# Two attention mixers of a transformer block on one NeuronCore: heads handled in pairs instead of one by one, and two weight staging buffers instead of three

## The chip, the cores and the metric

The kernel runs on one core of a Trainium2 chip. The metric is the time of one execution on the device, in microseconds (us). All data are float32, for a sequence of 512 tokens and a model width of 1024.

## What is computed

Two stacks are run one after the other, each of two layers. The change touches the mixer of the first stack alone. There a normed input `h` goes through one wide projection into queries, keys and values of two mixers and into gates:

```python
qa, ka, va, qb, kb, vb, gate_pre = jnp.split(h @ w_in[l], splits, axis=-1)
o_a = dilated_mixture(...)            # 12 heads of 64: 3 groups (window, dilation) x 4 slots
o_b = stick_breaking_attention(...)   # 4 heads of 64
merged = g_a * (o_a @ w_br[l, :OUT_A]) + g_b * (o_b @ w_br[l, OUT_A:])
```

Stick-breaking attention has no softmax. For a query t and a key s < t the weight is `sigmoid(z_ts) * prod(1 - sigmoid(z_tj))` over the keys j between them, so a running product along the keys is needed. The dilated mixture is softmax attention in three patterns, whose outputs are joined per slot by their softmax sums. The rest of the block is the output projection, a gated feed-forward net with a short convolution, and then the second stack (gated linear attention, differential attention, a Fourier mix and a feed-forward net, on the 512 tokens and, in part, on 256 context tokens).

## The kernel before

**Projections.** Nearly all the time goes into projections of weights that stream from HBM. `load_weights` (L116) brings each tile of 1024 columns x 128 rows of float32 (512 KB) into a buffer of the pool `raw` (L55, three buffers; L125, issued on SyncE's queue, SP). ScalarE then rounds it into `whi` (L126, three buffers), and VectorE writes the rest, `raw - whi`, into `wlo` (L127, two buffers); after that the `raw` buffer is free. `mm3` (L131 to L135) makes one product of three matmuls, `whi` by the input's high part, `whi` by its low part, `wlo` by its high part. `proj_t` (L137) does that for eight blocks of the contraction: 24 matmuls of 512 columns for one weight tile. `weights` (L106) asks for the next tile of a recorded plan while the current one is used.

**The mixer** (`mixer1`, L269) projects the stick-breaking queries and keys (L318, L319), then values (L328), then the twelve query and key tiles of the dilated mixture (L333, L334), then more values (L335). Then come the heads, one at a time: for each of four values of `s`, `stick(s)` (L536) and `dsw(s)` (L467). After them the softmax sums are exchanged through DRAM (`dsw_join`, L506), the outputs are transposed (`heads_t`, L561), sixteen gate tiles are projected (L351 to L360), and the branch projections begin (L366).

**stick** goes through four blocks of 128 queries. For each it makes a score matmul with a contraction of 64, from the upper or the lower half of the partitions (L545, `sc`), tanh on ScalarE (L547), then on VectorE a mask, the stay factors, a running product and the weights (L549 to L556), then transposes the weights block by block (L458, `at`), copies them out, on ScalarE or VectorE in turn (`evac`), and multiplies them with the values, with the transposed weights as the stationary side and 64 columns of values as the moving side (L464, `po`). **dsw** does the same with three scores for each of four query blocks (L478), a fused add-and-minimum and an exp (L487, L488), transposes (L494) and products with 65 columns of values (L500).

**Order.** The kernel gives only dependences and a program order. A scheduler in the framework fixes each engine's order at build time: on TensorE the next ready instruction, earliest in the program first. So the gate projections (`mm<-h`) stand between the heads' matmuls. Engines then run their queues in that fixed order. The banks of PSUM in this stage are `mm` 2, `sc` 3, `at` 2 and `po` 1 (L264). float32 matmuls that are not split appear in the trace as two records each, transposes as one.

Of the kernel before, what the change touches and what calls it, by code (L numbers as in the profile page):

```python
# [10 lines left out]
F32 = mybir.dt.float32  # L11
F32R = mybir.dt.float32r
U8 = mybir.dt.uint8
AF = mybir.ActivationFunctionType
ALU = mybir.AluOpType
# [3 lines left out]
P = 128  # L19
# [28 lines left out]
class Net:  # L48
    def __init__(self, ctx, tc, io, plan):
        self.plan, self.asked, self.ahead = plan, [], []  # L50
        self.tc, self.nc, self.io = tc, tc.nc, io
        pool = lambda name, bufs, **kw: ctx.enter_context(tc.tile_pool(name=name, bufs=bufs, **kw))
        self.pc = pool("const", 1)
        self.px = pool("resid", 1)
        self.praw = pool("raw", 3)  # L55
        self.pw = pool("wsplit", 1)
        self.ps = pool("tmp", 4)
        self.psm = pool("small", 4)
        self.n = 0
        self.consts()  # L60
# [19 lines left out]
    def tmp(self, name, n=T, dt=F32):  # L80
        if n <= TC:
            return self.ps.tile([P, n], dt, tag="th", name=self.nm(name), bufs=4)
        return self.ps.tile([P, n], dt, tag="t", name=self.nm(name))
# [147 lines left out]
    def token_factor(self, acc, classes=False):  # L231


        bc, r = self.rstd_bcast(acc, 4, D)
        if classes:
            r = r, self.rstd_cols(acc, 4, D, classes=True)
        out = self.pv1.tile([P, T], F32, tag="fac", name=self.nm("fac"), bufs=1)
        self.nc.scalar.copy(out, bc)
        return out, r
# [18 lines left out]
    def block1(self, layers, ctx=True):  # L258
        self.x = []
        with self.scope(pa=("act", 16), pv1=("factor", 1)):  # L260
            self.vec1 = self.pv1.tile([P, self.io["vec1"].shape[1]], F32, tag="vec1", name="vec1", bufs=1)
            self.nc.sync.dma_start(self.vec1, self.io["vec1"])
            for l in range(layers):
                with self.scope(pk=("work", 3), pv=("vals", 1), banks={"mm": 2, "sc": 3, "at": 2, "po": 1}):  # L264
                    acc = self.mixer1(l, None if l else "load")
                with self.scope(pmod=("mod", 2), banks={"mm": 6, "at": 2}):
                    self.ffn1(l, acc, ctx and l == layers - 1)

    def mixer1(self, l, first):  # L269
        nc, io = self.nc, self.io  # L270
        ready = []
        if first:
# [3 lines left out]
            for i in range(4):  # L276
                w = self.weights(io["w_in_t"][l, 12 + i], KT, P)
                if i == 0:
                    self.load_x(1, KT)
                    self.h1 = [self.gained(l, "norm1", k) for k in range(KT)]  # L280
                if i == 2:
                    for k in range(KT):
                        self.sumsq(self.acc1, self.x[k], k == 0)
                    self.load_consts()
                    fac, rcs = self.token_factor(self.acc1, True)
                ps = self.bank("mm" if i < 2 else "sc")
                self.proj_t(ps, w, 0, self.h1)
                ready.append(ps)
# [3 lines left out]
        self.nw = 0  # L292
# [33 lines left out]
        banks = ("mm", "mm", "sc", "sc")  # L326
# [6 lines left out]
        qa = proj_qk(0, 6, 0.125)  # L333
        ka = proj_qk(6, 6, 1.0)  # L334
        for ps in self.wide(io["w_in_n"][l, 1], hs, [slice(b, T, 4) for b in range(4)], banks):  # L335
            pass
        for b in range(4):
            nc.scalar.mul(va[1][b][:, :, 0:64], heads(ps[b]), rcs[1][:, b:b + 1])

        ob = [self.pv.tile([P, 256], F32, tag=f"ob{b}", name=self.nm("onat")) for b in range(4)]  # L340
# [3 lines left out]
        for s in range(4):  # L344
            self.stick(s, qb, kb, vb, ob)
            self.dsw(s, qa, ka, va, sums, stat)
        on, last = self.dsw_join(sums, stat)
        ob = self.heads_t(ob, "o")
# [17 lines left out]
        for c in range(4):  # L366
            w = self.weights(io["w_br"][l, c], 4, 256)
            for j in range(2):
                n = 2 * c + j
                pa, pb = self.bank("sc"), self.bank("sc")  # L370
# [80 lines left out]
    def weighted(self, out, blocks, width):  # L451

        nc = self.nc
        for b0 in range(0, len(blocks), 4):
            grp = blocks[b0:b0 + 4]
            pt = self.bank("at")
            for i, (p_, v) in enumerate(grp):
                nc.tensor.transpose(pt[:, i * P:(i + 1) * P], p_, self.ident)  # L458
            pT = self.tmp("pT")
            n = len(grp) * P  # L460
            self.evac(self.nw, pT[:, :n], pt[:, :n])
            self.nw += 1
            for i, (p_, v) in enumerate(grp):
                nc.tensor.matmul(out[:, :width], pT[:, i * P:(i + 1) * P], v,  # L464
                                 start=b0 + i == 0, stop=b0 + i == len(blocks) - 1)

    def dsw(self, s, qa, ka, va, sums, stat):  # L467
# [3 lines left out]
        bias = self.pk.tile([P, 512], F32, tag="bias", name=self.nm("bias"), bufs=2)  # L471
        nc.sync.dma_start(bias, self.io["dswb"][s])
        for b in range(4):
            k0 = max(b - 1, 0) * P
            n0 = (b + 1) * P - k0
            r = 64 * (s % 2)
            ps = self.bank("sc")
            mm = lambda out, g, q, k: nc.tensor.matmul(out, qa[2 * g + s // 2][r:r + 64, q], ka[2 * g + s // 2][r:r + 64, k],  # L478
                                                       start=True, stop=True)
            own = slice(b * P, (b + 1) * P)  # L480
            mm(ps[:, 0:n0], 0, own, slice(k0, (b + 1) * P))
            for g in (1, 2):
                mm(ps[:, (g + 1) * P:(g + 2) * P], g, own, own)
            e = self.pk.tile([P, 512], F32, tag="e", name=self.nm("e"), bufs=2)
            for c, (sl, bi) in enumerate(((slice(0, n0), bias[:, 256 - n0:256]), (slice(256, 512), bias[:, 256:512]))):
                nm = stat[:, c, b, 0, s:s + 1]
                nc.vector.tensor_tensor_reduce(e[:, sl], ps[:, sl], bi, -1.0, 3.0e38, ALU.add, ALU.min, accum_out=nm)  # L487
                nc.scalar.activation(e[:, sl], e[:, sl], AF.Exp, bias=nm, scale=-1.0)  # L488
            blocks = [(0, e[:, i * P:(i + 1) * P], va[0][k0 // P + i][:, s, :]) for i in range(n0 // P)]
            blocks += [(1, e[:, (g + 1) * P:(g + 2) * P], va[1][b][:, 4 * (g - 1) + s, :]) for g in (1, 2)]  # L490
            n = len(blocks) * P
            pt = self.bank("at")
            for i, (_, p_, _) in enumerate(blocks):
                nc.tensor.transpose(pt[:, i * P:(i + 1) * P], p_, self.ident)  # L494
            pT = self.tmp("pT")
            self.evac(self.nw, pT[:, :n], pt[:, :n])
            self.nw += 1
            po = self.bank("po")
            for i, (c, _, v) in enumerate(blocks):
                nc.tensor.matmul(po[:, 65 * c:65 * (c + 1)], pT[:, i * P:(i + 1) * P], v,  # L500
                                 start=i in (0, len(blocks) - 2), stop=i in (len(blocks) - 3, len(blocks) - 1))
            po = po[:, 0:130].rearrange("p (c d) -> p c d", c=2)
            nc.scalar.copy(sums[b][:, :, s, :], po[:, :, 0:64])
            nc.vector.tensor_copy(stat[:, :, b, 1, s:s + 1], po[:, :, 64:65])
# [31 lines left out]
    def stick(self, h, qb, kb, vb, on):  # L536

        nc = self.nc  # L540
        j, r = h // 2, 64 * (h % 2)
        for qi in range(4):
            kw = (qi + 1) * P
            pz = self.bank("sc")
            nc.tensor.matmul(pz[:, :kw], qb[j][r:r + 64, qi * P:kw], kb[j][r:r + 64, 0:kw], start=True, stop=True)  # L545
            y = self.tmp("y")
            nc.scalar.activation(y[:, :kw], pz[:, :kw], AF.Tanh, scale=0.5)  # L547
            d = y[:, qi * P:kw]
            nc.vector.tensor_tensor(d, d, self.smask, ALU.min)  # L549
            g = self.pk.tile([P, T + 2], F32, tag="stay", name=self.nm("stay"), bufs=1)  # L550
            nc.gpsimd.memset(g[:, 0:1], 1.0)
            nc.vector.tensor_scalar(g[:, kw:0:-1], y[:, :kw], -0.5, 0.5, ALU.mult, ALU.add)
            c = self.tmp("left")
            nc.vector.tensor_tensor_scan(c[:, :kw], g[:, 0:kw], g[:, 0:kw], 1.0, ALU.mult, ALU.bypass)
            rev = c[:, kw - 1::-1] if kw == T else c[:, 0:kw][:, ::-1]
            nc.vector.scalar_tensor_tensor(y[:, :kw], y[:, :kw], 1.0, rev, ALU.add, ALU.mult)  # L556
            po = self.bank("po")
            self.weighted(po, [(y[:, i * P:(i + 1) * P], vb[:, i, h * 64:(h + 1) * 64]) for i in range(qi + 1)], 64)
            nc.scalar.copy(on[qi][:, h * 64:(h + 1) * 64], po[:, 0:64])

    def heads_t(self, on, name, classes=None):  # L561

        out = []
        for j in range(2):
            pts = []
            for part in (on, classes) if classes else (on,):
                pt = self.bank("at")
# [911 lines left out]
    def block2(self):  # L1479
        st = Stream("l", T, 0, self.x)  # L1480
        st.acc = self.acc1
        with self.scope(pcx=("ctx", 1), psm=("small2", 4)):
# [188 lines left out]
```

## Time and profile before

| | |
|---|---|
| three timed runs | 3258.72, 3259.57, 3263.57 us; median 3259.57 |
| the profiled execution | 3259.87 us, of which the span of the instructions is 3258.1 us |
| TensorE matmul, weight load | 98%, 82% of the span |
| VectorE, ScalarE, GpSimd | 62%, 42%, 2% |
| granted TensorE clock, mean | 0.996 of full speed |
| HBM | 367.57 MB, 113 GB/s over the span |

Busy time is the time in which an engine has at least one instruction in flight. Matmuls are pipelined, so the duration of one (about 390 ns for 512 columns) is longer than the distance from its start to the next one's start; distances of starts are what an instruction costs TensorE. A row of the timeline is a run of like instructions: start, length from the first start to the last end, engine, line, operation, tiles, shape and count.

### The profile page before, as it was taken

How to read it: one execution, taken by the hardware profiler on the slowest of the kernel's cores; microseconds unless marked ns; L12 is line 12 of the kernel's file. 1: busy time of each engine (PE TensorE's matmuls, PEld its weight loads, DVE VectorE, ACT ScalarE, POOL GpSimd, SP SyncE). 2: the span in 40 equal slices, each digit the busy share in tenths (PEclk: the TensorE clock that was granted, in tenths of full speed). 3: DMA queues.
4: the chain of work that ended last, by engine and by line, in shares of the span. 5: the costliest groups of instructions: out<-in, count | busy, mean ns of one | idle time of the engine just before them, and what ended most of it. 6: DMA issues, size and time to landing. Idle time of an engine off the chain costs nothing.

```text
span 3258.1 us, 46766 instructions
## 1 busy us (share of the span) xinstructions
PE 3196.9 (98%) x18808; PEld 2684.9 (82%) x18808; DVE 2009.5 (62%) x3320; ACT 1353.8 (42%) x2304; POOL 68.7 (2%) x213
## 2 busy tenths in 40 slices
PE   9999999999999999999999999999999999999998
PEld 7878888888878888889778788888898778888887
DVE  4366799663456799667767775333266677653335
ACT  3244433242234433346647654222244467542223
POOL 0000000000000000000100000000000100000000
PEclk9999999999999999999999999999999999999999
DMA  4213466433213466436242234332134522222333
GB/s 141 84 40 117 132 202 216 130 104 91 81 37 117 148 204 210 136 106 193 86 131 75 59 111 138 95 97 91 57 117 131 168 78 71 76 80 93 97 95 117
DMA packets 109226, 370.62 MB, mean 114 GB/s; under 512 B 13264, under 2 KB 18384, under 8 KB 109008
## 3 DMA queue, kind: packets, MB, share of 16 engines
q1 hardware_dynamic: 103824, 352.28, 34.8%
q0 software_dynamic: 5184, 15.34, 1.7%
q8 instruction: 148, 2.42, 0.3%
q14 instruction: 70, 0.57, 0.1%
HBM read 359.64 MB, written 7.93 MB: 113 GB/s over the span
## 4 chain that ended last, share of the span: by engine, by line
PE 91%; DVE 3%; ACT 3%; DMA 2%; issue 1%; SPq 0%; DVEq 0%; ACTq 0%
PE mm L133 24%; PE mm L135 24%; PE mm L134 24%; PE at L1258 2%; PE sc L478 1%; PE po L500 1%; PE ds L1236 1%; DVE wlo L127 1%; PE mm L170 1%; PE mm L171 1%; PE mm L172 1%; DMA raw<-w_in2v 1%; ACT whi L126 1%; PE sc L545 1%; PE at L1254 1%
## 5 line engine op out<-in xcount | busy, mean ns | idle before, releaser
L126 ACT CAST whi<-raw 128x1024 fp32r<-128x1024 f32 (+1 forms) x556 | 575.9, 1036 | 1194.3 <-PE mm L134 793.4
L127 DVE TENSOR_TENSOR wlo<-raw,whi 128x1024 fp32r<-128x1024 f32 (+1 forms) x556 | 666.8, 1200 | 317.3 <-PE mm L135 175.8
L133 PE MATMUL mm<-h,whi 128*128 128x512 f32 x1904 | 753.3, 396 | 12.4 <-ACT whi L126 7.9
L135 PE MATMUL mm<-h,wlo 128*128 128x512 f32 x1904 | 753.2, 396 | 0.1
L134 PE MATMUL mm<-h,whi 128*128 128x512 f32 x1904 | 750.2, 394 | 0.0
L133 PEld LDWEIGHTS mm<-h,whi 128*128 128x128 f32 x1904 | 358.6, 188 | 85.3 <-issue 7.9
L135 PEld LDWEIGHTS mm<-h,wlo 128*128 128x128 f32 x1904 | 358.2, 188 | 74.8 <-DVE wlo L127 2.0
L134 PEld LDWEIGHTS mm<-h,whi 128*128 128x128 f32 x1904 | 358.3, 188 | 71.5 <-issue 1.1
L135 PE MATMUL mm<-hid,wlo 128*128 128x512 f32 (+1 forms) x896 | 324.7, 363 | 3.2 <-DVE wlo L127 3.1
L133 PE MATMUL mm<-hid,whi 128*128 128x512 f32 (+1 forms) x896 | 324.9, 363 | 0.4 <-ACT whi L126 0.4
L134 PE MATMUL mm<-hid,whi 128*128 128x512 f32 (+1 forms) x896 | 325.0, 363 | 0.0
L135 PEld LDWEIGHTS mm<-hid,wlo 128*128 128x128 f32 x896 | 168.8, 189 | 31.4 <-DVE wlo L127 3.8
L133 PEld LDWEIGHTS mm<-hid,whi 128*128 128x128 f32 x896 | 168.8, 189 | 28.3 <-ACT whi L126 0.6
L134 PEld LDWEIGHTS mm<-hid,whi 128*128 128x128 f32 x896 | 168.9, 189 | 27.9 <-DVE hid L180 0.4
L133 PE MATMUL mm<-cat,whi 128*128 128x512 f32 (+1 forms) x512 | 187.1, 367 | 4.6 <-ACT cat L701 3.3
L135 PE MATMUL mm<-cat,wlo 128*128 128x512 f32 (+1 forms) x512 | 186.8, 366 | 0.0
L134 PE MATMUL mm<-cat,whi 128*128 128x512 f32 (+1 forms) x512 | 186.4, 365 | 0.0
L1399 DVE TENSOR_TENSOR silu<-silu,mm 128x512 f32<-128x512 f32 (+1 forms) x58 | 36.1, 623 | 223.2 <-PE mm L135 222.7
L674 DVE SCALAR_TENSOR_TENSOR junk<-wmod,c 128x1024 f32<-128x1024 f32 x96 | 116.8, 1217 | 4.2 <-DMA wmod<-w_mod 3.7
L674 DVE SCALAR_TENSOR_TENSOR wmod<-wmod,c 128x1024 f32<-128x1024 f32 x96 | 116.8, 1217 | 0.7
L133 PEld LDWEIGHTS mm<-cat,whi 128*128 128x128 f32 x512 | 97.4, 191 | 20.5 <-ACT cat L701 3.6
L134 PEld LDWEIGHTS mm<-cat,whi 128*128 128x128 f32 x512 | 97.2, 190 | 15.1
(484 smaller groups left out, 5166.8 us busy)
## 6 DMA issues: line engine op xcount, KB each, us to landing
raw<-w_fi SPq DMA_DIRECT2D x120, 512.0 KB, 3.6
wmod<-w_mod SPq DMA_DIRECT2D x96, 512.0 KB, 4.2
raw<-w_up SPq DMA_DIRECT2D x88, 512.0 KB, 3.7
raw<-w_in2t SPq DMA_DIRECT2D x76, 512.0 KB, 3.6
raw<-w_in_t SPq DMA_DIRECT2D x64, 512.0 KB, 3.6
raw<-w_fo SPq DMA_DIRECT2D x48, 512.0 KB, 3.6
raw<-w_down SPq DMA_DIRECT2D x32, 512.0 KB, 3.7
raw<-w_out SPq DMA_DIRECT2D x28, 512.0 KB, 3.6
```

What stands on the lines that cost most here:

```text
L126: nc.scalar.copy(hi, raw)
L127: nc.vector.tensor_tensor(lo, raw, hi.bitcast(F32), ALU.subtract)
L133: mm(out, lh, rh, start=start, stop=False)
L134: mm(out, lh, rl, start=False, stop=False)
L135: mm(out, ll, rh, start=False, stop=stop)
L170: mm(out[i], xh, hi, start=k == 0, stop=False)
L171: mm(out[i], xh, lo, start=False, stop=False)
L172: mm(out[i], xl, hi, start=False, stop=k == last)
L478: mm = lambda out, g, q, k: nc.tensor.matmul(out, qa[2 * g + s // 2][r:r + 64, q], ka[2 * g + s // 2][r:r + 64, k], start=True, stop=True)
L674: ins = nc.vector.scalar_tensor_tensor(o, w, 1.0, cs[v], ALU.mult, ALU.mult, accum_out=self.mods[l][v][:, j:j + 1])
L1258: mm(po[:, 0:64], wT[:, i * P:(i + 1) * P], vals[c0 + i][:, h * 64:(h + 1) * 64], start=c0 + i == 0, stop=c0 + i == nkb - 1)
L1399: nc.vector.tensor_tensor(s, s, ps[1][:, :n], ALU.mult)
```

## The change

- `raw` has two buffers, not three.
- `stick` and `dsw` take two heads at a time, `j` in 0, 1. The two heads' score matmuls are issued in turn, one contracting over partitions 0 to 63, the other over 64 to 127, and write two neighbouring banks of PSUM (`pair_bank`, 1024 columns).
- In `stick` the elementwise steps cover both heads in one instruction, except for the running product, which is one instruction for each head, in place. The transposed weights are now the moving side (128 columns), the values the stationary side (64 columns), and the two heads write partitions 0 to 63 and 64 to 127 of one bank. The result is already transposed, so `heads_t` isn't called for it.
- `dsw` keeps its count of score, transpose and value instructions.
- The banks are `mm` 2, `sc` one pair, `at` one pair, `po` 2. Work tiles `y` have two buffers, shared by `stick` and `dsw`; `stay`, `pT` and `bias` have one.
- The second set of values is projected before the query and key tiles of the dilated mixture. The copy of the token factor comes before the column sums by class.

The diff without moves of small pools and without the removed bodies, which are printed above:

```diff
@@ -52,7 +52,7 @@
-        self.praw = pool("raw", 3)
+        self.praw = pool("raw", 2)
@@ -232,10 +232,10 @@
+        out = self.pv1.tile([P, T], F32, tag="fac", name=self.nm("fac"), bufs=1)
+        self.nc.scalar.copy(out, bc)
...
-        out = self.pv1.tile([P, T], F32, tag="fac", name=self.nm("fac"), bufs=1)
-        self.nc.scalar.copy(out, bc)
@@ -261,9 +261,9 @@
-                with self.scope(pk=("work", 3), pv=("vals", 1), banks={"mm": 2, "sc": 3, "at": 2, "po": 1}):
+                with self.scope(pk=("work", 1), pv=("vals", 1), banks={"mm": 2, "sc": 1, "at": 1, "po": 2}):
...
-                with self.scope(pmod=("mod", 2), banks={"mm": 6, "at": 2}):
+                with self.scope(pmod=("mod", 2), psh=("half", 4), banks={"mm": 6, "at": 2}):
@@ -283,13 +283,12 @@
-                ps = self.bank("mm" if i < 2 else "sc")
+                ps = self.bank("mm" if i < 2 else "po")
...
-        self.nw = 0
@@ -323,29 +322,32 @@
-        banks = ("mm", "mm", "sc", "sc")
+        banks = ("mm", "mm", "po", "po")
...
-        qa = proj_qk(0, 6, 0.125)
-        ka = proj_qk(6, 6, 1.0)
...
-        ob = [self.pv.tile([P, 256], F32, tag=f"ob{b}", name=self.nm("onat")) for b in range(4)]
+        qa = proj_qk(0, 6, 0.125)
+        ka = proj_qk(6, 6, 1.0)
+        ob = []
...
-        for s in range(4):
-            self.stick(s, qb, kb, vb, ob)
-            self.dsw(s, qa, ka, va, sums, stat)
+        for j in range(2):
+            ob.append(self.stick(j, qb, kb, vb))
+            self.dsw(j, qa, ka, va, sums, stat)
...
-        ob = self.heads_t(ob, "o")
+        nat, ob = ob, []
+        for o in nat:
+            ob.append(self.pair("o"))
+            self.split(ob[-1], o)
@@ -367,7 +369,7 @@
-                pa, pb = self.bank("sc"), self.bank("sc")
+                pa, pb = (self.bank(("mm", "po")[j]) for _ in range(2))
@@ -448,60 +450,63 @@
...
+    def pair_tile(self, tag, bufs=1):
+        return self.pk.tile([P, 2, 512], F32, tag=tag, name=self.nm(tag), bufs=bufs)
+    def pair_bank(self, tag):
+        return self.bank(tag, 1024).rearrange("p (s c) -> p s c", s=2)
+    def turned(self, t, n):
...
+        pt = self.pair_bank("at")
+        pT = self.pair_tile("pT")
+        for i in range(2):
+            for k in range(n):
+                sl = slice(k * P, (k + 1) * P)
+                nc.tensor.transpose(pt[:, i, sl], t[:, i, sl], self.ident)
+        for i in range(2):
+            self.evac(i, pT[:, i, :n * P], pt[:, i, :n * P])
+        return pT
+    def dsw(self, j, qa, ka, va, sums, stat):
...
+        bias = self.pair_tile("bias")
+        nc.sync.dma_start(bias, self.io["dswb"][2 * j:2 * j + 2].rearrange("s p c -> p s c"))
...
+            ps = self.pair_bank("sc")
+            for g, cols, keys in ((0, slice(0, n0), slice(k0, (b + 1) * P)), (1, slice(n0, n0 + P), own),
+                                  (2, slice(n0 + P, n0 + 2 * P), own)):
+                for i in range(2):
+                    r = slice(64 * i, 64 * i + 64)
+                    nc.tensor.matmul(ps[:, i, cols], qa[2 * g + j][r, own], ka[2 * g + j][r, keys], start=True, stop=True)
+            e = self.pair_tile("y", 2)
+            for i in range(2):
+                s = 2 * j + i
+                for c, (sl, bi) in enumerate(((slice(0, n0), slice(256 - n0, 256)), (slice(n0, n0 + 2 * P), slice(256, 512)))):
+                    nm = stat[:, c, b, 0, s:s + 1]
+                    nc.vector.tensor_tensor_reduce(e[:, i, sl], ps[:, i, sl], bias[:, i, bi], -1.0, 3.0e38, ALU.add, ALU.min,
+                                                   accum_out=nm)
+                    nc.scalar.activation(e[:, i, sl], e[:, i, sl], AF.Exp, bias=nm, scale=-1.0)
+            n = n0 // P + 2
+            pT = self.turned(e, n)
...
+            for i in range(2):
+                s = 2 * j + i
+                vs = [(0, va[0][k0 // P + k][:, s, :]) for k in range(n - 2)]
+                vs += [(1, va[1][b][:, 4 * (g - 1) + s, :]) for g in (1, 2)]
+                for k, (c, v) in enumerate(vs):
+                    nc.tensor.matmul(po[:, 130 * i + 65 * c:130 * i + 65 * (c + 1)], pT[:, i, k * P:(k + 1) * P], v,
+                                     start=k in (0, n - 2), stop=k in (n - 3, n - 1))
+            po = po[:, 0:260].rearrange("p (s c d) -> p c s d", s=2, c=2)
+            nc.scalar.copy(sums[b][:, :, 2 * j:2 * j + 2, :], po[:, :, :, 0:64])
+            nc.vector.tensor_copy(stat[:, :, b, 1, 2 * j:2 * j + 2], po[:, :, :, 64])
@@ -533,38 +538,48 @@
...
+    def stick(self, j, qb, kb, vb):
...
+        po = self.bank("po")
...
+            pz = self.pair_bank("sc")
+            for i in range(2):
+                r = slice(64 * i, 64 * i + 64)
+                nc.tensor.matmul(pz[:, i, :kw], qb[j][r, qi * P:kw], kb[j][r, 0:kw], start=True, stop=True)
+            y = self.pair_tile("y", 2)
+            nc.scalar.activation(y[:, :, :kw], pz[:, :, :kw], AF.Tanh, scale=0.5)
+            d = y[:, :, qi * P:kw]
+            nc.vector.tensor_tensor(d, d, self.smask.unsqueeze(1).broadcast_to([P, 2, P]), ALU.min)
+            g = self.pair_tile("stay")
+            nc.gpsimd.memset(g[:, :, 0:1], 1.0)
+            nc.vector.tensor_scalar(g[:, :, kw - 1:0:-1], y[:, :, 1:kw], -0.5, 0.5, ALU.mult, ALU.add)
+            for i in range(2):
+                c = g[:, i, 0:kw]
+                nc.vector.tensor_tensor_scan(c, c, c, 1.0, ALU.mult, ALU.bypass)
+            nc.vector.scalar_tensor_tensor(y[:, :, :kw], y[:, :, :kw], 1.0, g[:, :, 0:kw][:, :, ::-1], ALU.add, ALU.mult)
+            pT = self.turned(y, qi + 1)
+            for k in range(qi + 1):
+                for i in range(2):
+                    h = 2 * j + i
+                    nc.tensor.matmul(po[64 * i:64 * i + 64, qi * P:kw], vb[:, k, h * 64:(h + 1) * 64], pT[:, i, k * P:(k + 1) * P],
+                                     start=k == 0, stop=k == qi, tile_position=(0, 64 * i))
+        o = self.pv.tile([P, T], F32, tag=f"ob{j}", name=self.nm("ob"))
+        nc.scalar.copy(o, po)
+        return o
...
+            for part, bank in ((on, "at"), (classes, "po")) if classes else ((on, "at"),):
+                pt = self.bank(bank)
```

## Rows read from the trace of the kernel before

**Rows 1.** The page, busy time of TensorE over the whole span, with its count.

```profile
PE 3196.9 (98%) x18808; PEld 2684.9 (82%) x18808; DVE 2009.5 (62%) x3320; ACT 1353.8 (42%) x2304; POOL 68.7 (2%) x213
```

**Rows 2.** Heads of both layers: window, length, busy us (count) per engine, clock.

```profile
144.61:248.54 103.93, 103.81 (x588) 77.85 (x587) 63.52 (x172) 43.37 (x105) 1.49 (x15) 1.00 0.14 40
868.97:973.00 104.03, 103.81 (x585) 77.35 (x584) 63.06 (x172) 43.16 (x105) 1.49 (x15) 1.00 0.12 39
```

**Rows 3.** Groups on TensorE, heads of layer 1: count, busy us, mean ns.

```profile
L133 PE MATMUL mm<-h,whi 128*128 128x512 f32 x51 | 21.3, 418 | 0.0
L464 PE MATMUL po<-vb,pT 128*128 128x64 f32 x80 | 11.5, 275 | 0.0
L569 PE MATMUL at<-cmat,onat 128*128 128x128 f32 x8 | 1.2, 273 | 0.0
```

**Rows 4.** Timeline of TensorE around two groups of scores.

```profile
147.63 0.40 PE L134 MATMUL mm<-h,whi 128*128 128x512 f32 x1
147.95 1.12 PE L545 MATMUL sc<-qk,qk 64*128 64x512 f32 x2
149.01 0.50 PE L135 MATMUL mm<-h,wlo 128*128 128x512 f32 x1
...
150.21 0.48 PE L135 MATMUL mm<-h,wlo 128*128 128x512 f32 x1
150.62 0.93 PE L478 MATMUL sc<-qk,qk 64*128 64x128 f32 x6
151.48 0.50 PE L133 MATMUL mm<-h,whi 128*128 128x512 f32 x1
151.82 0.39 PE L134 MATMUL mm<-h,whi 128*128 128x512 f32 x1
152.05 0.40 PE L135 MATMUL mm<-h,wlo 128*128 128x512 f32 x1
```

**Rows 5.** Timeline of TensorE around one group of stick value products.

```profile
239.21 0.40 PE L133 MATMUL mm<-h,whi 128*128 128x512 f32 x1
239.46 1.07 PE L464 MATMUL po<-vb,pT 128*128 128x64 f32 x8
240.37 0.50 PE L494 MATMUL at<-cmat,e 128*128 128x128 f32 x3
```

**Rows 6.** Timeline of TensorE, second stack, matmuls in column quarters.

```profile
1738.36 0.48 PE L135 MATMUL mm<-h,wlo 128*128 128x512 f32 x1
1738.77 0.46 PE L1059 MATMUL lev<-q,As 128*32 128x32 f32 x32
1739.15 0.50 PE L133 MATMUL mm<-h,whi 128*128 128x512 f32 x1
```

**Rows 7.** Instructions of the joined outputs: first and last start.

```profile
L532 DVE TENSOR_TENSOR on<-sum,joint x8: 414/415/424, 258.5 to 260.8; 128x256 f32<-128x256 f32 x8
...
L133 PEld LDWEIGHTS sc<-o,whi x64: 186/188/188, 304.0 to 1050.0; 128*128 128x128 f32 x64
```

**Rows 8.** Roundings of weight tiles (L126): window, length, busy us (count).

```profile
1470.00:1546.00 76.00, 25.40 (x26) 1.00 0.61 188
1926.00:1996.00 70.00, 24.34 (x24) 1.00 0.56 171
2412.00:2470.00 58.00, 21.00 (x20) 1.00 0.61 187
3207.00:3236.00 29.00, 10.03 (x12) 1.00 0.52 162
```

**Rows 9.** Tile raw, one such stretch: ns min/median/max, first and last start.

```profile
L126 ACT CAST whi<-raw x5: 1033/1052/1056, 2428.2 to 2439.8; 128x1024 fp32r<-128x1024 f32 x5
L127 DVE TENSOR_TENSOR wlo<-raw,whi x5: 1215/1217/1219, 2428.4 to 2439.5; 128x1024 fp32r<-128x1024 f32 x5
L125 SPq DMA_DIRECT2D raw<-w_fi x5: 327/328/328, 2429.7 to 2440.8; - x5
...
DMA to landing us min/median/max: 3.5/3.8/4.2
```

More of the change, by code (lines that the diff above doesn't have):

```diff
@@ L81, in tmp @@
         if n <= TC:
-            return self.ps.tile([P, n], dt, tag="th", name=self.nm(name), bufs=4)
+            return self.psh.tile([P, n], dt, tag="th", name=self.nm(name), bufs=4)
         return self.ps.tile([P, n], dt, tag="t", name=self.nm(name))
@@ L449, in ffn1 @@
         self.modulation(l, before)
-    def weighted(self, out, blocks, width):
-        nc = self.nc
[L454 to L467, printed above, removed]
+    def pair_tile(self, tag, bufs=1):
[3 more added lines that the diff above has]
+    def turned(self, t, n):
+        nc = self.nc
+        pt = self.pair_bank("at")
[8 more added lines that the diff above has]
+    def dsw(self, j, qa, ka, va, sums, stat):
         nc = self.nc
-        bias = self.pk.tile([P, 512], F32, tag="bias", name=self.nm("bias"), bufs=2)
-        nc.sync.dma_start(bias, self.io["dswb"][s])
+        bias = self.pair_tile("bias")
+        nc.sync.dma_start(bias, self.io["dswb"][2 * j:2 * j + 2].rearrange("s p c -> p s c"))
         for b in range(4):
@@ L475, in dsw @@
             n0 = (b + 1) * P - k0
[L476 to L479, printed above, removed]
             own = slice(b * P, (b + 1) * P)
-            mm(ps[:, 0:n0], 0, own, slice(k0, (b + 1) * P))
-            for g in (1, 2):
-                mm(ps[:, (g + 1) * P:(g + 2) * P], g, own, own)
@@ L484, in dsw @@
[L484 to L497, printed above, removed]
-            po = self.bank("po")
-            for i, (c, _, v) in enumerate(blocks):
-                nc.tensor.matmul(po[:, 65 * c:65 * (c + 1)], pT[:, i * P:(i + 1) * P], v,
-                                 start=i in (0, len(blocks) - 2), stop=i in (len(blocks) - 3, len(blocks) - 1))
@@ L502, in dsw @@
-            po = po[:, 0:130].rearrange("p (c d) -> p c d", c=2)
-            nc.scalar.copy(sums[b][:, :, s, :], po[:, :, 0:64])
-            nc.vector.tensor_copy(stat[:, :, b, 1, s:s + 1], po[:, :, 64:65])
+            ps = self.pair_bank("sc")
[4 more added lines that the diff above has]
+                    nc.tensor.matmul(ps[:, i, cols], qa[2 * g + j][r, own], ka[2 * g + j][r, keys], start=True, stop=True)
@@ L534, in dsw_join @@
         return on, last
-    def stick(self, h, qb, kb, vb, on):
+    def stick(self, j, qb, kb, vb):
         nc = self.nc
-        j, r = h // 2, 64 * (h % 2)
+        po = self.bank("po")
         for qi in range(4):
             kw = (qi + 1) * P
[L544 to L559, printed above, removed]
@@ L565, in heads_t @@
             pts = []
-            for part in (on, classes) if classes else (on,):
-                pt = self.bank("at")
+            for part, bank in ((on, "at"), (classes, "po")) if classes else ((on, "at"),):
+                pt = self.bank(bank)
                 for b in range(4):
@@ L1481, in block2 @@
         st.acc = self.acc1
-        with self.scope(pcx=("ctx", 1), psm=("small2", 4)):
+        with self.scope(pcx=("ctx", 1), psm=("small2", 4), psh=("half", 4)):
             self.consts2()
```

## The prediction

> **What bounds the kernel now.** I read the page first. TensorE has a matmul in flight for 98% of the span [rows 1], so only work taken from TensorE, or a new wait of TensorE, can change the time. Next come the windows over the two stretches in which the heads run. TensorE is just as full there, at full clock, while VectorE is busy 63 of 104 us and ScalarE 43 [rows 2]. The heads are therefore not bound by their own chain of scores, tanh, products and transposes. When that chain waits, gate projections fill TensorE. The groups by line show how much: 51 matmuls of L133 in layer 1's stretch [rows 3], and as many of L134 and L135 within one or two, since the three alternate; 151 in all. Two neighbours start 0.23 us apart [rows 4], so the fill is 151 x 0.23 = 34.7 us, and the heads themselves take 103.9 - 34.7 = 69 us of TensorE per layer. That is what the change can shrink. A 0.2% difference, 6.5 us, is about what a measurement of this kernel can tell from none.
>
> **Scores.** The price of a group is the distance between the projections around it, less 0.23 us for the projection before it [rows 4]. A stick group of two records of 512 columns costs 149.01 - 147.63 - 0.23 = 1.15 us. A dsw group of six records of 128 costs 151.48 - 150.21 - 0.23 = 1.04 us. 256 columns more cost 0.11 us, which gives 0.43 ns a column and a fixed 0.71 us a group, much of it spent changing the shape in which the array is used. A head has four stick groups (2560 columns in two records each) and four dsw groups (768 + 3 x 1024 columns): 8 x 0.71 + 6400 x 0.00043 = 8.4 us, or 33.7 us for four heads. In pairs there are half as many groups. If the two row halves work side by side, a pair costs what one head costs now, 16.9 us per layer: 16.8 us less. Some groups stand next to each other already and share the fixed part, so I take off 3 us and use 14. If the halves take turns, the columns cost the same and only some fixed parts go; I put the lower end at 0.
>
> Do tiles of the array work side by side? No row shows two row halves at once. The nearest rows are the column quarters of the second stack: 32 records between 1738.77 and 1739.15, 12 ns each [rows 6], against 114 ns for a record on the whole array (0.91 us for eight) [rows 5]. That is far too fast for taking turns, so I use the value at the side of full overlap.
>
> The Trainium skill has a rule against this, in "TensorE: Matmul & The Clock Gate", section "The mechanism" of the part on packing small matmuls: matmuls are strict first in, first out, in start and in end. By that rule the second record of head one holds up head two, and the sum would be that of the rival "in turn by records" below. The quarters in [rows 6] do not look like it.
>
> **Stick's value products.** Now 80 records a layer [rows 3] at 0.114 us [rows 5]: 9.1 us. Afterwards 80 records of 128 moving columns, two halves of the columns side by side, and eight more changes of the array's shape. For a record of 128 columns I take 0.13 us, the dsw group's 1.04 us over six with some of its fixed part left in [rows 4]. For a change I take 0.3 us, since a whole group of quarters costs 1739.15 - 1738.36 - 0.23 = 0.56 us with 32 records in it [rows 6]. 40 x 0.13 + 8 x 0.3 = 7.6 us saves 1.5. Without overlap it is 12.8, which costs 3.7; at the column price of 0.43 ns it is 4.6, which saves 4.5.
>
> **Transposes and joint steps.** `heads_t` for stick loses its 8 transposes a layer [rows 3], at about 0.1 us each 0.9 us. All other transposes and dsw's value products keep their count: nothing. The joint elementwise steps remove fixed parts of instructions on VectorE and ScalarE, which are not the bound: nothing, and the cover is their idle 40 us in [rows 2].
>
> **Single buffers.** Scores, transposes, `stay` and `pT` now have one place for a pair, so the next scores wait for the tanh or for dsw's minimum, and the next transposes for both copies. Behind a waiting score in TensorE's fixed order stand gate matmuls, so a wait in the wrong place stops TensorE for a moment. As a whole the chain has room. The heads end at 248.5, the joined outputs are there at 260.8, and the branch projections that need them begin at 304.0 [rows 2, 7]. About 40 us of other projections lie between, per layer, and fill a longer chain. If that cover went, each us of chain would cost a us. I cost this at nothing, with up to 5 us a layer as its upper end. The earlier copy of the token factor and the new order of the value projection move no work: nothing, with the same cover.
>
> **Two raw buffers.** A raw buffer is held from the issue of its load until VectorE has subtracted. At the usual pace a weight tile feeds 24 matmuls, 24 x 0.23 = 5.5 us. A load lands in 3.8 us, rounding takes 1.05 and subtraction 1.22 [rows 9]; with 0.2 for handing over, 6.3 us, so two buffers sustain a tile every 3.1 us. That is hidden behind 5.5. It is not hidden where 256 tokens make a tile last half as long: 70 tiles in 204 us, one every 2.9 us, and 12 tiles in 29 us at the end [rows 8], where tiles are smaller by a quarter (about 2.4 us with two buffers, an estimate from the same rows, against 2.4 now). The price is (3.14 - 2.91) x 70 = 16 us, less what tiles rounded in advance cover: two on entry to each of three stretches could cover all of it. Between 0 and 16 I take 10, because [rows 9] shows waiting besides: five roundings in 11.6 us are 2.9 us apart, so three buffers turn over in 8.7 us, not 6.3. If all that waiting stayed, two buffers would give a tile every 4.35 us. The upper end is then 1.44 x 70 + 1.2 x 12 = 115 us. Behind a raw load that waits on SP stand the other loads of SP, and they have the same slack as the tiles.
>
> **Sum.** Per layer 14 + 1.5 + 0.9 = 16.4 us less, 33 us for two, and 10 us more for the raw buffers. The profiled execution took 3259.9 us, 0.3 above the median of the three runs: 3259.9 - 33 + 10 = 3236.9, so 3237 us.
>
> **Rivals.**
> - *The halves overlap, as forecast*: 3237 us, with 3216 (22 us a layer saved, raw free) to 3253 (raw at 16, 5 us a layer of waits) as its own range. Chance 0.58.
> - *In turn by records*: each product is two records on the same half, and the next head's first record starts only beside the second. Then a stick pair takes 3 of 4 slots and a dsw pair 7 of 12, which saves 0.25 x 15.8 + 0.42 x 17.9 = 11.5 us less the same 3. With 2.4 for the rest that is 11 us a layer: 3259.9 - 22 + 10 = 3248 us. For it speaks that no row shows two halves, against it [rows 6]. Chance 0.16.
> - *The change doesn't do what it says: halves strictly one after the other*. Only fixed parts of half the groups are saved, at most 16 x 0.71 = 11 us, and I take 6; value products cost 3.7 more, transposes 0.9 less. About 3 us a layer: 3259.9 - 6 + 10 = 3264 us. Chance 0.12.
> - *Slower: the raw buffers decide*. In the stretches of [rows 8] the hold time stays as it is, since VectorE subtracts no sooner. With 33 us gained and 115 lost, 3342 us. It outweighs the gain from 33/82 = 0.4 us a tile, which is a hold time of 6.6 us. For it speaks that the forecast leaves only 0.3 us to that point. Against it: when tiles come later, VectorE has less queued, and its subtraction no longer waits for a `wlo` buffer. Chance 0.14, a part of it just past break-even.
>
> **Numbers.** The likeliest case gives 3237. The range reaches down to 3216 and up to the case without overlap, 3264; outside lie most of the last rival and the ends of the others, together under 0.2. Below 3253 lie nearly all of the first case and most of the second: faster 0.70. Between 3253 and 3266 lie the third and the edges: same 0.15. Slower 0.15.
>
> **What would show it.** In the heads' stretches, scores of two heads with starts a few ns apart, and a pair's group near 1.1 us. A heads stretch with 17 us less TensorE time of its own and the same 384 gate matmuls a layer. In the four stretches of [rows 8], tiles up to 3.1 us apart, with TensorE waiting for `whi` or `wlo` where it didn't. Groups near 2 us refute the overlap. A stretch longer by over 0.4 us a tile refutes the raw price. TensorE idle just before the branch projections refutes the cover of the chain.

## The result, and the profile after

The change makes the kernel **slower**: 3285.62 us in the median of four runs (3284.81 to 3286.37) beside 3259.14 for the kernel before. The ratio is 1.0078, with a 95% interval of 1.0061 to 1.0096, so about 26 us are lost where 23 were to be gained. Later runs had the kernel before at 3262.5 to 3263.6 us beside them; I compare by ratio and turn ratios into us with 3259.

The page of the changed kernel: the span, busy times (the line that answers to [rows 1]), and the chain of work that ended last.

```profile
span 3284.6 us, 46618 instructions
...
PE 3200.1 (97%) x18792; PEld 2674.0 (81%) x18792; DVE 2000.4 (61%) x3256; ACT 1350.6 (41%) x2246; POOL 68.8 (2%) x197
...
PE 73%; DVE 11%; DMA 10%; ACT 4%; issue 1%; ACTq 0%; SPq 0%; DVEq 0%
```

TensorE's busy time did not fall. The chain tells more. Its line in the page before is

```profile
PE 91%; DVE 3%; ACT 3%; DMA 2%; issue 1%; SPq 0%; DVEq 0%; ACTq 0%
```

The end of the kernel now hangs on transfers (DMA) and on VectorE, which subtracts, far more often.

**The heads** got shorter. The windows from a layer's first score to the end of its last value product (length, then busy us and count of TensorE, its weight load, VectorE, ScalarE and GpSimd, clock, DMA):

```profile
145.98:230.80 84.82, 82.89 (x521) 58.65 (x521) 52.93 (x135) 35.47 (x70) 1.67 (x7) 1.00 0.10 32
866.75:953.27 86.52, 84.42 (x521) 59.77 (x521) 52.93 (x135) 35.46 (x70) 1.67 (x7) 0.98 0.10 31
```

92 projections of 0.23 us lie between them, so the heads' own time is 84.8 - 21.2 = 63.7 and 86.5 - 21.2 = 65.4 us. Over the same bounds before (103.6 and 104.3 us with 150 projections) it is 69.1 and 69.8. The gain is 5.4 and 4.4 us a layer, where the forecast had 16.4. And TensorE, which was idle for 0.1 and 0.2 us in [rows 2], now stands for 1.9 and 2.1 us. The granted clock is 0.98 in layer 2, which is about 1.7 us of its 86.5 and the difference between the two layers.

**Weight tiles** got slower. The roundings of the same tiles as in [rows 8] (one less in the first two, by the bounds), in windows from their first to just after their last:

```profile
1472.00:1556.00 84.00, 25.52 (x25) 1.00 0.53 163
1939.00:2014.00 75.00, 24.15 (x23) 0.98 0.53 158
2429.00:2492.00 63.00, 20.61 (x20) 1.00 0.54 168
3228.00:3262.00 34.00, 10.01 (x12) 1.00 0.49 146
```

From the first of these roundings to the last it is 82.8, 73.4, 62.3 and 32.4 us; the same tiles before took 75.1, 64.9, 56.1 and 25.0. That is 30 us lost in four places. TensorE's weight load names the wait (wait, total us, times, longest): of the kernel before

```profile
PEld mm L133 <- ACT whi L126: 8.3, 4, 6.8
PEld mm L135 <- DVE wlo L127: 7.9, 12, 2.1
```

and of the changed kernel

```profile
PEld mm L135 <- DVE wlo L127: 26.9, 51, 1.3
PEld mm L133 <- ACT whi L126: 17.3, 10, 6.9
```

All weight-load waits for `whi` and `wlo` together grew from 22.9 to 56.7 us.

**The order on TensorE.** A timeline in layer 1 of the changed kernel shows a pair of stick scores of 384 columns (L553):

```profile
151.35 0.44 PE L467 MATMUL at<-cmat,y 128*128 128x128 f32 x2 [0.49 <-DVE y L565]
151.72 0.91 PE L553 MATMUL sc<-qk,qk 64*128 64x384 f32 x2
152.56 0.44 PE L570 MATMUL po<-pT,vb 128*64 128x128 f32 x4
152.92 0.91 PE L553 MATMUL sc<-qk,qk 64*128 64x384 f32 x2
153.76 0.50 PE L134 MATMUL mm<-h,whi 128*128 128x512 f32 x1
```

The two heads' products don't meet: value products stand between them. TensorE takes instructions in a fixed order, and in that order 24 of the 64 score pairs of the two layers are split like this, among them all four of 512 columns.

### The profile page after: what moved, and what is told of

It reads as the page before. It is cut to its first block, busy times and chain, and to the rows that moved or that the text cites. A ratio compares the mean times of both kernels' runs of the same rounds, so it can differ in the third digit from the quotient of the medians.

```text
span 3284.6 us, 46618 instructions
## 1 busy us (share of the span) xinstructions
PE 3200.1 (97%) x18792; PEld 2674.0 (81%) x18792; DVE 2000.4 (61%) x3256; ACT 1350.6 (41%) x2246; POOL 68.8 (2%) x197
## 4 chain that ended last, share of the span: by engine, by line
PE 73%; DVE 11%; DMA 10%; ACT 4%; issue 1%; ACTq 0%; SPq 0%; DVEq 0%
PE mm L135 19%; PE mm L133 19%; PE mm L134 19%; DVE wlo L127 3%; DMA raw<-w_up 3%; ACT whi L126 2%; DVE junk L689 2%; DMA raw<-w_fi 2%; DMA wmod<-w_mod 1%; DVE wmod L689 1%; PE at L1273 1%; DMA raw<-w_in2t 1%; DMA raw<-w_fo 1%; PE po L505 1%; DMA raw<-w_in2v 1%
## 5 line engine op out<-in xcount | busy, mean ns | idle before, releaser
L126 ACT CAST whi<-raw 128x1024 fp32r<-128x1024 f32 (+1 forms) x556 | 576.0, 1036 | 1282.3 <-PE mm L134 282.7
L133 PEld LDWEIGHTS mm<-cat,whi 128*128 128x128 f32 x512 | 96.2, 189 | 18.8 <-ACT cat L716 2.9
L135 PEld LDWEIGHTS mm<-cat,wlo 128*128 128x128 f32 x512 | 96.4, 189 | 15.4 <-DVE wlo L127 0.4
```

Of the source, the lines that this page charges most:

```text
L126: nc.scalar.copy(hi, raw)
L133: mm(out, lh, rh, start=start, stop=False)
L135: mm(out, ll, rh, start=False, stop=stop)
```

## Experiments

**Theory A**: two raw buffers cost about 40 us, and the heads gave 13, because split pairs cannot overlap. **Theory B**: the raw buffers cost the 10 us of the prediction, and the paired heads lost the rest.

**1. The kernel before with two raw buffers.**

```
-        self.praw = pool("raw", 3)
+        self.praw = pool("raw", 2)
```

> The kernel before with two raw buffers in place of three, nothing else. Theory A (two raw buffers cost about 40 us, and the paired heads gave 13): 3259 + 40 = 3299 us, 3293 to 3305. Theory B (the raw buffers cost about 10 us, as the prediction has it, and the paired heads lost the rest): 3269 us, 3264 to 3275.

Measured: 1.0128 (1.0113 to 1.0144), or +42 us. Its weight-load waits:

```profile
PEld mm L135 <- DVE wlo L127: 32.7, 50, 1.7
PEld mm L133 <- ACT whi L126: 16.8, 13, 6.8
```

This one line, without any pairing, costs what theory A says. B falls.

**2. The changed kernel with three raw buffers.**

```
-        self.praw = pool("raw", 2)
+        self.praw = pool("raw", 3)
...
-        bias = self.pair_tile("bias")
+        bias = self.gtile("bias", (P, 2, 512))
```

> The changed kernel with three raw buffers again; the room for the third comes from taking the pair's bias tile from the pool of the gates. Theory A: 3286 - 40 = 3246 us, 3240 to 3252, so faster than before by what the heads gave. Theory B: 3286 - 10 = 3276 us, still slower than before. If the borrowed buffer delays the gates, a TensorE wait for a gate's tile would show behind the heads and the time would be above A's.

Measured: 0.9956 (0.9943 to 0.9968), 14 us faster than before and 40 faster than the changed kernel. The windows of the same tiles' roundings are back; from the first to the last it is 75.8, 65.1, 55.8 and 25.7 us:

```profile
1457.00:1534.00 77.00, 25.72 (x26) 1.00 0.60 183
1916.00:1982.00 66.00, 23.40 (x23) 1.00 0.57 173
2399.00:2456.00 57.00, 21.03 (x20) 1.00 0.64 190
3195.00:3223.00 28.00, 10.03 (x12) 1.00 0.49 152
```

And so are the weight-load waits:

```profile
PEld mm L133 <- ACT whi L126: 10.8, 6, 6.6
PEld mm L135 <- DVE wlo L127: 5.6, 7, 2.1
```

Both kernels do the same heads, so the ends of the same tile's subtraction can be compared through the whole run. The changed kernel falls behind by 9 us before 1442 us (4 in layer 1 and 5 in layer 2, where a tile lasts 5 us and more), by 28.5 within the four windows, counted from their first rounding to their last, and ends 37 behind by the spans. In the first window the lag is large at once: it is 9.3 us up to three tiles before it and 14 to 17 us in its first four tiles. Of the 5 us in layer 2, 2.3 fall into the heads, whose windows in experiment 2 are both at full clock:

```profile
145.73:229.95 84.22, 82.79 (x521) 58.61 (x521) 52.98 (x135) 35.35 (x70) 1.67 (x7) 1.00 0.09 26
862.59:946.82 84.23, 82.76 (x521) 58.61 (x521) 52.98 (x135) 35.35 (x70) 1.67 (x7) 1.00 0.08 26
```

**3 and 4. The score pairs bound together**, in the changed kernel, and with the edit of experiment 2. The second head's product gets a priority ahead of the other work and an order edge (no wait) to the first; the same in `stick`:

```
-                    nc.tensor.matmul(ps[:, i, cols], ...)
+                    with self.tc.high_priority() if i else ExitStack():
+                        ins = nc.tensor.matmul(ps[:, i, cols], ...)
+                    if i:
+                        self.after(ins, first)
+                    first = ins
```

> The changed kernel with the second head's score product bound directly behind the first head's on TensorE in all 64 pairs; in the changed kernel 24 of the 64 have other work between them. Theory A with the split pairs as the reason why the heads gave only 13 us: a split pair costs the duration of one product more than a joined one, some 1.0 us at 512 columns (4), 0.75 at 384 (2), 0.5 at 256 (8), 0.25 at 128 (10): 4 + 1.5 + 4 + 2.5 = 12 us, so 3274 us, 3268 to 3280. Rival (TensorE waits for the elementwise chain anyway and the order gives nothing): 3283 to 3289 us.

> Both edits: three raw buffers and the score pairs bound together. Theory A with the split pairs: 3286 - 40 - 12 = 3234 us, 3227 to 3241, below both kernels. If the order gives nothing: 3246 us. Theory B: 3264 us or more.

Measured: 1.0050 (1.0037 to 1.0062) and 0.9932 (0.9920 to 0.9945), so 9 and 8 us better than the same kernels unbound, of 12 expected, and with three raw buffers 22 us faster than before. The four 512-column pairs are now of this kind (joined kernel with three raw buffers, timeline of layer 1):

```profile
152.79 0.40 PE L133 MATMUL mm<-h,whi 128*128 128x512 f32 x1
153.12 1.13 PE L559 MATMUL sc<-qk,qk 64*128 64x512 f32 x4
154.18 0.66 PE L467 MATMUL at<-cmat,y 128*128 128x128 f32 x4
```

Four records take 154.18 - 153.12 = 1.06 us, as long as one head's two did in [rows 4]. In the trace the first records of both heads start 6 ns apart, and so do the second ones.

**5. Joined pairs that read the same row half** (three raw buffers; the second head's scores are then the first head's). In `dsw` the rows change likewise.

```
-    nc.tensor.matmul(pz[:, i, :kw], qb[j][r, qi * P:kw], kb[j][r, 0:kw], ...)
+    nc.tensor.matmul(pz[:, i, :kw], qb[j][0:64, qi * P:kw], kb[j][0:64, 0:kw], ...)
```

> Three raw buffers and joined pairs, but both heads' score products read the first head's 64 rows, so the two products of a pair stand side by side and cannot share the array (the second head's scores are thus the first head's; the work is the same in number and size). Theory A with overlap of the row halves: the score products of a layer go back from about 17 us of TensorE time to about 28 us, as they have in the kernel before, so 2 x 11 = 22 us above the joined version, 1.000 of the kernel before (0.998 to 1.002). Rival (the second product is cheap for another reason, its place right behind the first alone): as the joined version, 0.993.

Measured: 0.9973 (0.9964 to 0.9982), 13 us above the joined version, not 22, but clear of the rival's 0.993. The same pair:

```profile
153.44 1.98 PE L559 MATMUL sc<-qk,qk 64*128 64x512 f32 x4
155.35 0.33 PE L467 MATMUL at<-cmat,y 128*128 128x128 f32 x1
```

1.91 us: on one half the products take turns. The groups by line for the scores of layer 1 (count, busy us, mean ns, idle before), first in the kernel before:

```profile
L478 PE MATMUL sc<-qk,qk 64*128 64x128 f32 (+1 forms) x96 | 17.9, 316 | 0.1
...
L545 PE MATMUL sc<-qk,qk 64*128 64x128 f32 (+3 forms) x32 | 12.6, 478 | 0.0
```

In the changed kernel:

```profile
L488 PE MATMUL sc<-qk,qk 64*128 64x128 f32 (+1 forms) x96 | 14.4, 334 | 0.0
...
L553 PE MATMUL sc<-qk,qk 64*128 64x128 f32 (+3 forms) x32 | 10.8, 482 | 0.3 <-ACT y L555 0.3
```

In the joined kernel of experiment 4:

```profile
L489 PE MATMUL sc<-qk,qk 64*128 64x128 f32 (+1 forms) x96 | 11.2, 334 | 0.0
...
L559 PE MATMUL sc<-qk,qk 64*128 64x128 f32 (+3 forms) x32 | 6.5, 482 | 0.0
```

And in this one:

```profile
L489 PE MATMUL sc<-qk,qk 64*128 64x128 f32 (+1 forms) x96 | 17.7, 316 | 0.0
...
L559 PE MATMUL sc<-qk,qk 64*128 64x128 f32 (+3 forms) x32 | 10.7, 456 | 0.0
```

Scores: 30.5 us before, 25.2 as built, 17.7 joined, 28.4 on one half. The overlap is worth 28.4 - 17.7 = 10.7 us a layer, 21 for two, yet the time shows 13. The windows of the heads tell where the rest goes. In the joined kernel:

```profile
145.87:220.45 74.58, 71.39 (x502) 51.49 (x502) 51.78 (x135) 35.62 (x70) 0.99 (x7) 1.00 0.07 22
857.39:933.49 76.10, 72.87 (x502) 52.56 (x502) 51.98 (x135) 35.62 (x70) 0.99 (x7) 0.98 0.07 22
```

In experiment 5, whose other layer has a row like this one:

```profile
145.39:226.21 80.82, 80.80 (x502) 60.23 (x502) 52.12 (x135) 35.48 (x70) 0.99 (x7) 1.00 0.07 20
```

With the slow scores TensorE is hardly ever idle (0.02 us); with the overlapped ones it stands for 3.2 us a layer, 2.0 of them before stick's value products, which wait for a copy of the transposes (`pT`). The heads' own chain has come out from behind the scores. Layer 2 of the joined kernel has a granted clock of 0.98 besides, about 1.5 of its 76.1 us. Whether a second `pT` would shorten the wait was not tested.

**6 and 7. Raw buffers in halves.** The room stays; each weight tile comes in two loads, two roundings and two subtractions. First in the changed kernel (four halves in the room of two), then with three buffers' room and joined pairs (six halves). Here `ks` and `cs` pick the half, and the lines for a whole tile, which these replace, are left out:

```
+            for i in range(2):
...
+                raw = self.praw.tile([P, k2, c2], F32, tag="raw", name=self.nm("raw"))
+                nc.sync.dma_start(raw, src[:, k0 + ks.start:k0 + ks.stop, cs])
+                nc.scalar.copy(hi[:, ks, cs], raw)
+                nc.vector.tensor_tensor(lo[:, ks, cs], raw, hi[:, ks, cs].bitcast(F32), ALU.subtract)
```

> The changed kernel with its raw room cut in four halves in place of two whole tiles: the same bytes, each weight tile brought, rounded and subtracted in two halves. Theory A (a buffer is held for the landing and for a rounding and a subtraction, and the number of buffers over that time sets how fast tiles come): a half is held some 5 us, 3.5 of landing and 0.6 + 0.7 of elementwise work, so four give a whole tile each 2.5 us, under the 3.1 us that TensorE asks for; most of the 40 us come back, 3246 to 3260 us on a chip where before takes 3259, a ratio of 0.996 to 1.000, with at most 560 more roundings and subtractions as the price. Rival (the bytes in flight decide): as the changed kernel, 1.006 to 1.010.

> Six half raw buffers (the room of three), and joined pairs. Theory A: not above the version with three whole raws and joined pairs, 0.991 to 0.994 of the kernel before; if the additional elementwise instructions hold up the residual and gate work, 0.996.

Measured: 1.0013 (1.0005 to 1.0022) and 0.9911 (0.9895 to 0.9926). With the same bytes, 21 of the 40 us come back, so the count of buffers matters and not the bytes alone; the expected 26 or more do not. Over the tiles of the three long stretches a half is held 6.2 to 6.9 us on average, not 5, because its subtraction begins 2.3 to 2.4 us after the rounding's start, though the rounding takes 0.62.

**8. A third `wlo`**, the changed kernel with two whole raws.

```
-                               for t, b in (("whi", 3), ("wlo", 2))]
+                               for t, b in (("whi", 3), ("wlo", 3))]
...
-        bias = self.pair_tile("bias")
+        bias = self.gtile("bias", (P, 2, 512))
```

> The changed kernel with two raw buffers and a third buffer for the rounded-off parts (wlo); the bias tile from the gates' pool again. In the short-tile stretches of the changed kernel a raw is held 7.0 to 7.4 us and the subtraction begins 1.5 to 2.0 us after the rounding, of which the rounding is 1.05. If the subtraction is late because both wlo buffers are still in use by TensorE, a third takes some 0.4 to 0.9 us off the hold, half of that off a tile's pitch, over 80 tiles 16 to 36 us: a ratio to the kernel before of 0.997 to 1.003. If it is late because VectorE is at other work or was told late, nothing changes: 1.006 to 1.010.

Measured: 1.0030 (1.0018 to 1.0042), the edge of the first range, but not in the way it said. In the four stretches the mean hold is 7.0, 6.6, 6.7 and 6.3 us, and it was 7.0, 6.6, 6.6 and 5.8: not shorter anywhere. Yet some 16 us are gained (20 between the two profiled executions), and TensorE's weight load waits less:

```profile
PEld mm L133 <- ACT whi L126: 14.2, 7, 6.9
PEld mm L135 <- DVE wlo L127: 7.6, 12, 1.5
```

By the starts of TensorE's projections, taken in order and measured against experiment 2, the changed kernel loses 9.1 us from the first head to 1440 us, 12.6 up to 1912, 6.6 up to 2390 and 8.6 after; with a third `wlo` it is 1.8, 4.0, 4.0 and 8.4. Raw tiles come no faster, but a tile more can lie finished ahead of need; that this is the reason is my reading, and no run separates it.

**9. The kernel before with six half raws.** The loop of experiment 6, in the kernel before.

> The kernel before with six half raw buffers in the room of its three, to see how much of the last version's gain comes from the finer buffers alone. Finer buffers gave the joined version about 7 us (0.9932 to 0.9911); if they do so whatever the heads do, 0.996 to 0.999 of the kernel before. If three whole raws are enough for the kernel before and the additional instructions cost, 1.000 to 1.003.

Measured: 1.0000 (0.9991 to 1.0009). Finer buffers give nothing where three whole ones are enough. The difference between experiments 7 and 4 (0.9911 and 0.9932, with intervals that meet) is therefore not put down to them.

**10. Half raws and a third `wlo`** in the changed kernel: the edits of 6 and 8.

> The changed kernel with four half raw buffers and a third wlo buffer. With half raws alone the ratio was 1.0013, a half was held 6.2 to 6.7 us, and its subtraction began 1.9 to 2.5 us after the rounding, which takes 0.62. If the subtraction waits there for a wlo that TensorE still reads, a third one shortens the hold to some 5 us and the rest of the loss goes too: 0.994 to 0.998, as with three whole raws. If VectorE is late for another reason, or the bytes in flight limit, 1.000 to 1.003.

Measured: 0.9966 (0.9952 to 0.9979), as with three whole raws. Over the same tiles the subtraction now begins 1.0 to 1.7 us after the rounding's start, and TensorE's waits for `wlo` fall to 5.7 us, from 17.8 with half raws alone. The hold, 6.1 to 6.4 us, hardly fell and not to the expected 5: what the subtraction no longer waits, the landed half mostly waits before its rounding (0.7 to 1.6 us, from 0.2 to 0.5). I take that wait to belong to tiles that are ahead of need, which no run shows. By the time, the third `wlo` gives back the rest of the loss where the raws are finer.

## Why the prediction was wrong

**The overlap of the row halves: right, though the sign I took for it was weak.** "A pair costs what one head costs now" holds for joined pairs: 1.06 us at 512 columns, 1.91 on one half. But [rows 6] did not show it as said. At the prediction's own 0.43 ns a column, a record of 32 columns would cost 14 ns when taking turns, so 12 ns each is not "far too fast" for that; I had compared with records of 64 columns. That price was off as well: records of 512 columns on one half start 0.43 us apart in experiment 5, 0.84 ns a column, so the fixed part of a group is smaller than 0.71 us. The total of 33.7 us a layer came out near the 30.5 us of busy time all the same. The rival "in turn by records", drawn from the Trainium skill ("TensorE: Matmul & The Clock Gate", section "The mechanism"), would have 3 of 4 slots. The second head did not wait for the first head's second record: the heads' records alternate, and each pair starts together. Whether that departs from the rule's order of instructions, the trace can't tell, since it doesn't say which record belongs to which instruction.

**The score term of 14 us a layer: the step that failed is that a pair of products in the program is a pair on TensorE.** I never asked what the fixed order would put between two heads. The score groups fell by 5.3 us in layer 1; bound together they fall by 12.8, near the 14. The heads' own time in experiment 2 is 63.1 us in both layers (84.2 less 92 x 0.23), and 57.8 and 59.3 when joined (74.6 and 76.1 less 73 x 0.23). Splitting costs these 5.3 + 3.8 = 9.1 us, about the 8 measured. The lower figure belongs to the layer with the granted clock of 0.98; with its 1.5 us put back, both layers give 5.3.

**"Single buffers: nothing": within its bounds, but not nothing.** TensorE idles 1.9 to 2.1 us a layer as built and 3.2 when joined. The wait that is plainly for a buffer, scores behind the tanh, is 0.3 to 0.4 us a layer as built; how much of the rest the single buffers cause was not tested. I looked for cover at the far end of the chain, where it is (the joined outputs are there at 244.5 us, the branch projections begin at 299.6), and not in TensorE's order, where no other work was placed just ahead of the waiting instruction. Of the 16.4 us forecast per layer, 6.0 and 6.7 came (experiment 2, from 69.1 and 69.8), 5.3 a layer went to split pairs, 3.2 is what the joined kernel still idles, and 1.9 and 1.2 stay unassigned.

**Value products and transposes: mechanism right.** The 80 stick value products fell from 11.5 us in [rows 3] to 8.7 in layer 1, more than the 1.5 forecast; in the trace the two heads' records start 7 ns apart. The 8 transposes are gone.

**Two raw buffers, "I take 10": the term that turned the sign.** It measures 40 to 42 us, between its bounds of 0 and 115 and far from the value taken. Three steps of it failed:
- *The hold of 6.3 us.* It was made of medians with 0.2 us for handing over. Over the tiles of the four windows the mean hold is 7.0, 6.6, 6.6 and 5.8 us, and half of it is the pitch within 0.1 us: 3.45, 3.34, 3.28 and 2.95 measured (3.13, 2.95, 2.95 and 2.27 before). The landings' mean is 3.7 to 4.1 us in the three long stretches, 0.1 to 0.3 pass before the rounding, and 0.2 to 0.5 between rounding and subtraction. So a tile costs 0.3 to 0.4 us there, and 0.7 in the last stretch, which I had even (2.4 against 2.4).
- *"Tiles rounded in advance cover."* They did not: in experiment 2's comparison the lag is there from the first tiles of the first stretch. A third `wlo` brought cover back there (experiment 8).
- *"Hidden behind 5.5."* Where a tile lasts that long, 9 us were lost all the same, some 1.7 of them by the lower clock in layer 2's heads. The weight load's waits for `wlo` in the changed kernel are 4.0 us in nine between 280 and 720 us, and 3.4 in seven between 1000 and 1442, where experiment 2 has none.

The rival "raw buffers decide" named the mechanism, the places and the break-even of 0.4 us a tile. The time fell there: 30 us over 80 tiles is just under 0.4 each, and with over half of the heads' gain missing that was enough. I gave it 0.14, because I read "hold 6.3, break-even 6.6" as a margin; it is none when the hold is an estimate with 0.2 us of slack.

What stays open: the 1 to 2 us a layer above.

## What to carry to other kernels

Price a buffer cut in the stretch with the shortest tiles: mean hold over buffers, against the pitch (the time from one tile's rounding to the next), with every wait inside the hold, and read a small margin there as a coin toss. Instructions that shall run side by side must stand side by side in the engine's order: look at that order, or bind them, before counting the gain. When TensorE work gets cheaper, look next at what feeds it; here 3 us a layer of the chain came out, and the version with joined pairs and the raw room of three, 0.9911 to 0.9932 of the kernel before, beats both kernels.

## What the runs showed of the hardware

The clock fell behind a series of short stalls. TensorE's windows of 3 us in the second stretch of the changed kernel (length, busy and count, granted clock, DMA):

```profile
1982.00:1985.00 3.00, 2.12 (x19) 1.00 0.48 164
1985.00:1988.00 3.00, 3.00 (x21) 0.75 0.62 179
1988.00:1991.00 3.00, 3.00 (x20) 0.68 0.47 173
```

After several windows with stalls, the last with 0.88 us idle, the granted clock is at the lower of its two levels (1.2 of 2.4 GHz) in parts of the next two. The same projections of 256 columns start 0.12 us apart before it falls and 0.21 after:

```profile
1986.18 0.28 PE L134 MATMUL lev<-hid,whi 128*128 128x256 f32 x1
1986.30 0.28 PE L135 MATMUL lev<-hid,wlo 128*128 128x256 f32 x1
...
1988.05 0.41 PE L135 MATMUL lev<-hid,wlo 128*128 128x256 f32 x1
1988.26 0.41 PE L133 MATMUL lev<-hid,whi 128*128 128x256 f32 x1
```

In these two windows 41 matmuls start, where full windows have 26 to 28 each. In experiment 2 the clock over this stretch is 1.00. Some 1.5 us of the stretch's 8.5 are thus lost at the lower clock (13 matmuls less, at 0.12 us); that the stalls brought it on is likely and not shown. The mean over the span is the same 0.995 in both. In the heads, too, idle time alone doesn't tell when the clock falls: the joined kernel idles 3.2 us in each layer, and its clock is 1.00 in one and 0.98 in the other.

Leaving the shape of 64 rows costs too: in the kernel before, a score of 128 columns followed by a record on the whole array takes 0.20 us to the next start, against 0.13 on average before another score.
